# Output projection wholly in Strassen form by way of DRAM, with its operands and those of the first FFN product made in two parts; norm powers on ScalarE and the attention mask ahead of the exponential

## The chip, the cores and the metric

One core of one Trainium2 chip runs the whole layer as one program. The metric is the device time of that core in microseconds (us). Five engines work side by side, each through its own queue in order: TensorE (PE, with its weight loads as PEld), VectorE (DVE), ScalarE (ACT), GpSimd (POOL) and SyncE (SP), which here only issues DMA transfers. Operands live in SBUF, matmul results in PSUM banks, weights and spilled tensors in DRAM. All values are float32.

## The reference

512 tokens (T), a model width of 2048, one layer of a decoder with two parallel branches:

```python
h = rmsnorm(x, attn_norm_g)
proj = h @ w_in                       # u, v_sgu, q, k, v_att, g_a, g_b
u = gelu(u); v_sgu = rmsnorm(gelu(v_sgu), sgu_norm_g)
y_a = u * (tril(w_s) @ v_sgu + b_s)   # per chunk of 128 tokens
q = rmsnorm(q, q_norm_g); k = rmsnorm(k, k_norm_g)     # per head of 128
...
z = q @ k.T * Dh ** -0.5
strict = key_pos < q_pos
log_1m = where(strict, log_sigmoid(-z), 0)
tail = cumsum(log_1m, reverse=True) - log_1m
w = where(strict, exp(log_sigmoid(z) + tail), 0)
y_b = w @ v
...
merged = sigmoid(g_a) * (y_a @ w_up_a) + sigmoid(g_b) * (y_b @ w_up_b)
x = x + merged @ w_o
hid = rmsnorm(x, ffn_norm_g) @ w_ffn_in
x = x + (silu(hid[..., :HID]) * hid[..., HID:]) @ w_ffn_out
x = x + sigmoid(rmsnorm(x, ple_norm_g) @ w_ple_gate) * (p @ w_ple)
```

The changed parts are the norms of q and k, the masked weights w, `merged @ w_o` and the product with `w_ffn_in`.

## The kernel before, in words

Activations are kept transposed. A large product is cut into *forms* and *units*. A form is the moving operand of 256 rows of the contracted dimension (a `Form`, with 512 tokens); a unit, or *pair*, is 256 output columns, and walks over all forms of the product (8 for the model width). Every float32 matrix product is made of three matmuls with the operands split into a high part (ACT, a rounding copy, `whi` or `parts`) and the rest (DVE, a subtraction, `wlo` or `parts`).

For each form a unit uses one of two kinds. Kind **P** (plain): four blocks of weights, 12 matmuls of 512 columns. Kind **S** (Strassen): seven products of half blocks. Undoubled, an S form takes 21 matmuls of 256 columns (`mm3`, lines 284 to 286). *Doubled* (line 695), each product needs 7 matmuls of 512 and 7 of 256 columns, since the high part of the weight meets the high and low halves of the operand side by side; the halves are then added by `mix_doubled`. Doubling needs a PSUM bank for each product, and is used only where a unit holds no P form.

The operand of an S form needs seven blocks in place of four: the first four are those of a P form too, the other three are sums. A form can be made at once (`strassen_form`, `all_first`) or in two parts (`plain_first`): first the four blocks, with which units take it as P, and then, after a second load of the same rows, the three sums. The table `until` says for how many units a form is still taken as P. Two arenas of SBUF hold the operands: `parts` for split operands (an S form takes 3584 columns of 29,696) and `wholes` for raw ones.

What sets the order: the code walks the units, and `tick()`, called once for each form of a unit on PE, lets the other work in. At a tick at most one raw operand is fetched, one form of the list `builds` steps on, and steps that `after(n, ...)` put off come due. Weights come in through SP into four landing places, the sums of S weights by an accumulating DMA on POOL and by DVE (line 363), their high parts on ACT (line 347), their rests on DVE (line 344), into three slots; a slot is free when PE is done with the pair of forms that used it.

The stages in turn: the input projection (36 units; the attention runs beside it in four rounds), the up projections with gates (`w_up_a`, `w_up_b`, all P), the output projection (8 units `j` over the 8 forms `ms`), five small products of the per-layer embedding (`ple_pair`), FFN-in (44 units `m` over the 8 forms `fs`), FFN-out in three passes, and the last gate.

Before the change the output projection takes its forms by `OUT = "SSSSPPPP"` in each unit, from `merged[j]` in SBUF. FFN-in takes unit 0 as P and all others as doubled S, with its forms (loaded from the spilled `x1`) made at once. FFN-out already has its forms from DRAM in two parts: unit 0 all P, unit 1 half S and half P, and doubled S from unit 2 (`PLAIN_UNTIL`).

In the attention each of 32 blocks (a head and 128 keys, four rounds of eight) goes through `stage_a` (scores, logarithms), `stage_m` (DVE makes `w` and `s`, POOL masks `s`), `stage_b` and `stage_c` (split of the sums), `stage_d` (two matmuls with a triangle, `w` minus their result, exponential, POOL mask of `w`), and after four blocks `finish` (matmuls with `v`). The norms of q and k take squares on ACT, a mean on DVE, the power -0.5 on POOL, for q a factor on DVE, and scale the tokens on ACT.

## Time and profile before

| what | before |
|---|---|
| median of 3 runs | 2675.95 us (2674.31 to 2677.8) |
| the profiled execution, its own time | 2676.21 us |
| its span in the trace | 2674.5 us |
| granted TensorE clock | 0.999 |
| busy share PE, DVE, ACT, POOL | 99%, 82%, 52%, 18% |
| DMA moved | 540.25 MB, 202 GB/s over the span |
| up projections on PE | 825.8 to 1001.1 us |
| output projection on PE | 1001.1 to 1169.2 us |
| five embedding products, then FFN-in unit 0 | 1169.2 to 1182.7, to 1209.4 us |
| rest of FFN-in on PE | to 2048.7 us |

Times are read from the start of the span. Matmuls overlap on PE, so the distance between the starts of two of them is the cost of one, not its length. A unit's cost is the distance between the first matmuls of two units. A row of waits gives the engine and line that waited, for whom, the total in us, how often, and the longest.

### The profile page before, as it was taken

Reading aid. Unit: us, or ns where it says so; the run is one execution under the profiler, and the core shown is the slowest. Engines: PE = TensorE matmul, PEld = TensorE weight load, DVE = VectorE, ACT = ScalarE, POOL = GpSimd, SP = SyncE. Lnnn points to the kernel's source line nnn. Section 1 sums busy time; section 2 is a strip of 40 time slices with the busy share of each in tenths; the row PEclk is TensorE's granted clock in tenths of the full one; section 3 lists DMA queues with packets and bytes.
Section 4 is the critical chain, followed back from the end, with each engine's and each line's share of the span. In section 5 each row is a group of like instructions: output and inputs, shape, how many; then the busy total and the mean of one; then the engine's idle time right before and its main releaser. Section 6 shows DMA issues by size and latency. Waiting matters only on the chain.

```text
span 2674.5 us, 42586 instructions
## 1 busy us (share of the span) xinstructions
PE 2647.8 (99%) x15496; PEld 2322.1 (87%) x15496; DVE 2206.1 (82%) x3720; ACT 1392.0 (52%) x2171; POOL 471.2 (18%) x565
## 2 busy tenths in 40 slices
PE   8999999999999999999999999999999999999999
PEld 7889898988998889988888888888888888889898
DVE  8587878787887666678888888888889989989776
ACT  7656565665554334365444444444445445445543
POOL 0232323232220000001111111111111211211010
PEclk9999999999999999999999999999999999999999
DMA  7577777777776457668888888888788989978784
GB/s 230 151 186 175 180 173 184 173 179 201 178 187 199 141 154 210 188 213 195 220 217 206 207 202 201 204 202 206 195 208 226 263 219 272 226 238 257 242 241 132
DMA packets 285939, 540.25 MB, mean 202 GB/s; under 512 B 25632, under 2 KB 138016, under 8 KB 285728
## 3 DMA queue, kind: packets, MB, share of 16 engines
q1 hardware_dynamic: 224624, 424.25, 49.0%
q0 software_dynamic: 61104, 113.27, 27.0%
q8 instruction: 121, 1.98, 0.3%
q14 instruction: 90, 0.74, 0.1%
HBM read 490.24 MB, written 47.19 MB: 201 GB/s over the span
## 4 chain that ended last, share of the span: by engine, by line
PE 89%; DVE 5%; ACT 2%; DMA 2%; issue 1%; POOL 1%; SPq 0%; DVEq 0%; ACTq 0%; POOLq 0%
PE ps L695 48%; PE ps L286 11%; PE ps L285 11%; PE ps L284 11%; PE small L695 6%; DVE wlo L344 1%; DVE out L754 1%; PE small L1157 1%; DMA wholes<-x 1%; PE small L1032 1%; DVE wholes L363 1%; ACT whi L347 1%; DVE parts L275 0%; PE small L1107 0%; POOL wholes L1120 0%
## 5 line engine op out<-in xcount | busy, mean ns | idle before, releaser
L695 PE MATMUL ps<-parts,whi 128*128 128x512 f32 x3960 | 1324.8, 397 | 0.3 <-DVE p L754 0.3
L347 ACT ACTIVATE whi<-wholes 128x512 fp32r<-128x512 f32 (+3 forms) x933 | 866.5, 942 | 785.1 <-DVE wholes L363 270.9
L344 DVE TENSOR_TENSOR wlo<-wholes,whi 128x512 fp32r<-128x512 f32 (+3 forms) x933 | 974.4, 1078 | 82.5 <-ACT whi L347 82.1
L695 PEld LDWEIGHTS ps<-parts,wlo 128*128 128x128 f32 x3960 | 743.7, 188 | 167.8 <-issue 1.0
L695 PE MATMUL ps<-parts,wlo 128*128 128x256 f32 x3960 | 784.3, 279 | 0.1
L285 PE MATMUL ps<-parts,whi 128*128 128x256 f32 (+1 forms) x2070 | 678.3, 328 | 1.0 <-DVE parts L275 0.9
L286 PE MATMUL ps<-parts,wlo 128*128 128x256 f32 (+1 forms) x2070 | 677.9, 328 | 1.1 <-DVE wlo L344 1.1
L284 PE MATMUL ps<-parts,whi 128*128 128x256 f32 (+1 forms) x2048 | 668.0, 328 | 8.2 <-ACT parts L274 5.9
L695 PEld LDWEIGHTS ps<-parts,whi 128*128 128x128 f32 x3960 | 637.7, 189 | 6.1 <-issue 1.0
L285 PEld LDWEIGHTS ps<-parts,whi 128*128 128x128 f32 x2070 | 392.5, 190 | 41.4 <-DVE parts L275 2.5
L284 PEld LDWEIGHTS ps<-parts,whi 128*128 128x128 f32 x2048 | 388.2, 190 | 44.0 <-ACT parts L274 7.4
L286 PEld LDWEIGHTS ps<-parts,wlo 128*128 128x128 f32 x2070 | 392.8, 190 | 35.5 <-DVE wlo L344 2.3
L363 DVE TENSOR_TENSOR wholes<-wholes 128x256 f32<-128x256 f32 (+1 forms) x806 | 338.7, 420 | 21.3 <-DVE wlo L344 3.0
L754 DVE TENSOR_TENSOR out<-out,ps 128x256 f32<-128x256 f32 x460 | 190.5, 416 | 142.1 <-ACT out L751 141.8
L351 POOL DMA_DIRECT2D wholes<-w_ffn_in x172 | 150.1, 872 | 690.0 <-DVE wholes L363 268.5
L351 POOL DMA_DIRECT2D wholes<-w_in x132 | 117.8, 894 | 480.6 <-DVE wholes L363 125.9
L695 PE MATMUL small<-parts,whi 128*128 128x512 f32 x440 | 174.5, 397 | 0.0
L275 DVE TENSOR_TENSOR parts<-wholes,parts 128x1024 fp32r<-128x1024 f32 (+4 forms) x138 | 131.5, 965 | 18.9 <-ACT parts L274 18.9
L274 ACT ACTIVATE parts<-wholes 128x1024 fp32r<-128x1024 f32 (+4 forms) x138 | 113.2, 845 | 44.8 <-DVE wholes L513 25.7
L351 POOL DMA_DIRECT2D wholes<-w_ffn_out x64 | 55.9, 873 | 355.2 <-DMA wholes<-w_ffn_out 87.6
L751 ACT ACTIVATE out<-ps 128x256 f32<-128x256 f32 x243 | 91.0, 384 | 46.6 <-PE ps L695 43.3
L1403 ACT ACTIVATE out<-out 128x512 f32<-128x512 f32 x44 | 27.9, 633 | 159.6 <-DVE out L1402 159.6
(120 smaller groups left out, 1735.5 us busy)
## 6 DMA issues: line engine op xcount, KB each, us to landing
wholes<-w_ffn_in SPq DMA_DIRECT2D x172, 384.0 KB, 5.7
wholes<-w_in SPq DMA_DIRECT2D x132, 384.0 KB, 4.8
wholes<-w_ffn_in SPq DMA_DIRECT2D x172, 256.0 KB, 4.9
wholes<-w_ffn_in POOLq DMA_DIRECT2D x172, 256.0 KB, 5.4
wholes<-w_in SPq DMA_DIRECT2D x132, 256.0 KB, 4.1
wholes<-w_in POOLq DMA_DIRECT2D x132, 256.0 KB, 4.9
wholes<-w_ffn_out SPq DMA_DIRECT2D x64, 384.0 KB, 6.2
wholes<-hid SPq DMA_DIRECT2D x42, 512.0 KB, 6.1
```

The lines of the kernel that those rows point to most:

```text
L274: return (nc.scalar.activation(hi, src, AF.Copy), nc.vector.tensor_tensor(out=lo, in0=src, in1=hi.bitcast(F32), op=ALU.subtract))
L275: nc.vector.tensor_tensor(out=lo, in0=src, in1=hi.bitcast(F32), op=ALU.subtract))
L284: nc.tensor.matmul(ps, sh, mh, start=start, stop=False)
L285: nc.tensor.matmul(ps, sh, ml, start=False, stop=False)
L286: return nc.tensor.matmul(ps, sl, mh, start=False, stop=stop)
L344: in_turn(nc.vector.tensor_tensor(out=self.lo[:, blocks], in0=r, in1=h.bitcast(F32), op=ALU.subtract))
L347: in_turn(nc.scalar.activation(h, r, AF.Copy))
L351: nc.gpsimd.dma_start(out=raw[:, 3:5], in_=self.src[:, 1:3], accum_op=ALU.add)
L363: in_turn(nc.vector.tensor_tensor(out=o, in0=x, in1=y, op=ALU.add))
L695: m = nc.tensor.matmul(out, l, r, start=first and k == 0, stop=last and k == 1)
L751: in_turn(nc.scalar.activation(out, x, AF.Copy, scale=scale))
L754: in_turn(nc.vector.tensor_tensor(out=out, in0=x, in1=y, op=op))
```

## The change

- The output projection is all S: unit 0 takes its 8 forms as P, unit 1 four as S and four as P, units 2 to 7 all as S and doubled (`HALF`).
- Its operands go by way of DRAM: each `merged[j]` is stored, and a `late_form` loads it for the first four blocks and once more for the sums.
- FFN-in's forms are made in two parts in the same manner, with a second load and a second scaling by the norm's gain; its unit 1 is now half S and half P.
- `ple_operands` moves from unit 1 of the output projection to three ticks into unit 7.
- A second part is fetched only when no first part of its stage among the next three is still to be fetched, unless the form was used already.
- The norms of q and k take their power as a logarithm and an exponential on ACT; the factor of q is folded into the constants of the mean.
- The mask of `w` stands in `stage_m`, before the subtraction, with -10000 in place of 0 after the exponential.

```diff
-OUT = "SSSSPPPP"
+MASKED = -1e4
+
 PASSES = "SSSSSSSS", "SSSSSSSS", "SSSSPP"
-PLAIN_UNTIL = (1, 1, 1, 1, 2, 2, 2, 2), (1, 1, 1, 1, 2, 2, 2, 2), (2, 2, 2, 2, 1, 1)
+HALF = 1, 1, 1, 1, 2, 2, 2, 2
+PLAIN_UNTIL = HALF, HALF, (2, 2, 2, 2, 1, 1)
...
         elif seconds and fits([(wholes, 5 * 256, "old")]):
-            (urgent or seconds)[0].fetch_second()
+            f = (urgent or seconds)[0]
+            if f.used or not any(b.stage == f.stage and b.ready() and not b.there
+                                 for b in list(builds)[:AHEAD]):
+                f.fetch_second()
...
-    def token_rms(ps, r):
+    def token_rms(ps, r, scale=1.0 / P, eps=eps_cols):
 
         norm1.row()
         ms = squares(ps)
-        nc.vector.scalar_tensor_tensor(out=ms, in0=ms, scalar=1.0 / P, in1=eps_cols,
+        nc.vector.scalar_tensor_tensor(out=ms, in0=ms, scalar=scale, in1=eps,
                                        op0=ALU.mult, op1=ALU.add)
-        nc.gpsimd.tensor_tensor(out=r, in0=ms, in1=expo[:, :NT], op=ALU.pow)
+        nc.scalar.activation(ms, ms, AF.Ln)
+        nc.scalar.activation(r, ms, AF.Exp, scale=-0.5)
...
-            token_rms(ps, r)
-            nc.vector.tensor_scalar(out=r, in0=r, scalar1=float(P) ** -0.5, scalar2=None,
-                                    op0=ALU.mult)
+            token_rms(ps, r, 1.0, eps_q)
...
                 nc.gpsimd.memset(s[0:1, :P], 0.0)
+            nc.gpsimd.affine_select(out=w[:, :P], in_=w[:, :P], pattern=[[1, P]],
+                                    compare_op=ALU.is_gt, fill=MASKED, base=0,
+                                    channel_multiplier=-1)
...
             nc.scalar.activation(w, w, AF.Exp)
-            nc.gpsimd.affine_select(out=w[:, :P], in_=w[:, :P], pattern=[[1, P]],
-                                    compare_op=ALU.is_gt, fill=0.0, base=0,
-                                    channel_multiplier=-1)
...
-            plan(w_o[j], OUT)
+            plan(w_o[j], now("S" * KU, HALF, j))
...
-            plan(w_ffn_in[m], ("S" if m else "P") * KU)
+            plan(w_ffn_in[m], now("S" * KU, HALF, m))
...
+    def store(n, j, block):
+        nc.sync.dma_start(out=spill[n, j], in_=block.f())
+        there.add((n, j))
+        give(block)
+
+    ms = [spilled_form("S", "mix", j) for j in range(KU)]
+    build(ms)
...
-                merged[j] = s
-    finish_waiting()
+                after(1, lambda j=j, s=s: store("mix", j, s))
...
-    fs = [spilled_form("S", "x1", j, (g_ffn, j), twice=False) for j in range(KU)]
+    fs = [spilled_form("S", "x1", j, (g_ffn, j)) for j in range(KU)]
...
+        if j == KU - 1:
+            after(3, ple_operands)
         if j == 1:
-            ple_operands()
-            builds.extend(fs)
-        pr = pair(ms, last=j == KU - 1)
+            build(fs)
+        pr = pair(ms, last=j == KU - 1, j=j, until=HALF, doubled=7)
...
-        o = pair(fs, last=m == KH - 1, j=m, until=(1,) * KU, doubled=7).out()
+        o = pair(fs, last=m == KH - 1, j=m, until=HALF, doubled=7).out()
```

In the code after the change line numbers are other ones: 284 is the high part of an operand (274 before), 357 that of weights (347), 520 the scaling by a gain (508), 873 a copy of an embedding product out of PSUM (885), 361 the accumulating weight transfer (351), 1108 the select on `s` (1120), 1117 the select on `w` (1148), 1028 a square (1039), 1044 the scaling of tokens (1054).

POOL's queue in the attention, some blocks into the first round. Before:

```order
L351 DMA wholes<-w_in 128x512
L1148 AFFINE_SELECT wholes<-wholes 128x128
L1120 AFFINE_SELECT wholes<-wholes 128x128
L1127 COPY wholes<-wholes 1x384
L351 DMA wholes<-w_in 128x512
L1128 MEMSET wholes 1x128
```

After:

```order
L361 DMA wholes<-w_in 128x512
L1117 AFFINE_SELECT wholes<-wholes 128x128
L1108 AFFINE_SELECT wholes<-wholes 128x128
L1115 COPY wholes<-wholes 1x384
L361 DMA wholes<-w_in 128x512
L1116 MEMSET wholes 1x128
```

The rows look alike, but before, 1148 belongs to an earlier block, whose exponential it follows; after, 1117 is the mask of the very block whose select 1108 it now stands ahead of.

ACT's queue at the first norms of q and k. Before (`rr_819` is the power that POOL makes, `cols` the factors for v):

```order
L347 ACTIVATE whi_80<-wholes 128x1280
L1039 ACTIVATE sq_835,ms_834<-small_829 128x128
L347 ACTIVATE whi_80<-wholes 128x512
L1054 ACTIVATE wholes<-small_814,rr_819 128x128
L1054 ACTIVATE wholes<-small_842,cols_591 128x128 x4
L1054 ACTIVATE wholes<-small_814,rr_819 128x128 x3
```

After:

```order
L357 ACTIVATE whi_80<-wholes 128x1280
L1038 ACTIVATE ms_822<-ms_822 128x4
L1028 ACTIVATE sq_837,ms_836<-small_831 128x128
L1039 ACTIVATE rr_821<-ms_822 128x4
L357 ACTIVATE whi_80<-wholes 128x512
L1044 ACTIVATE wholes<-small_816,rr_821 128x128
L1044 ACTIVATE wholes<-small_845,cols_592 128x128 x2
```

The logarithm and the exponential (1038, 1039) stand between the high parts of weights.

ACT's queue late in unit 7 of the output projection and on into the embedding products. Before:

```order
L508 ACTIVATE wholes<-wholes,gcol 128x512
L347 ACTIVATE whi_80<-wholes 128x512
L508 ACTIVATE wholes<-wholes,gcol 128x512 x3
L274 ACTIVATE parts<-wholes 128x4x256 x2
L274 ACTIVATE parts<-wholes 128x3x256
L347 ACTIVATE whi_78<-wholes 128x512
L274 ACTIVATE parts<-wholes 128x3x256
```

After:

```order
L357 ACTIVATE whi_76<-wholes 128x512
L357 ACTIVATE whi_80<-wholes 128x512
L520 ACTIVATE wholes<-wholes,gcol 128x512 x2
L284 ACTIVATE parts<-wholes 128x512 x2
L284 ACTIVATE parts<-wholes 128x4x256
L357 ACTIVATE whi_78<-wholes 128x512
L520 ACTIVATE wholes<-wholes,gcol 128x512 x2
L739 ACTIVATE out_10710<-ps_10588 128x256
L284 ACTIVATE parts<-wholes 128x4x256
L739 ACTIVATE out_10710<-ps_10593 128x256
```

`whi_80` of 512 columns holds the weights of the first embedding product. The sums' high parts (3x256) have left this place and come later; the embedding's operands (128x512 x2) and the copies out of the doubled unit's PSUM banks (739) have come in.

76 lines of the change are left out of this document (31 added, 45 removed).

## The prediction

> **What bounds the kernel now.** First I read the page's busy times, slices and chain of waits.
>
> ```profile
> span 2674.5 us, 42586 instructions
> PE 2647.8 (99%) x15496; PEld 2322.1 (87%) x15496; DVE 2206.1 (82%) x3720; ACT 1392.0 (52%) x2171; POOL 471.2 (18%) x565
> ...
> PEclk9999999999999999999999999999999999999999
> ...
> PE 89%; DVE 5%; ACT 2%; DMA 2%; issue 1%; POOL 1%; SPq 0%; DVEq 0%; ACTq 0%; POOLq 0%
> ```
>
> PE is busy in nearly the whole span at the full granted clock, and the chain runs through it for 89%. A busy PE may still be slowed, so next I took what PE waited for, from the view of waits:
>
> ```profile
> PE ps L284 <- ACT parts L274: 5.9, 2, 4.8
> ...
> PE small L1032 <- ACT wholes L1054: 2.2, 1, 2.2
> PE small L1157 <- POOL wholes L1148: 2.2, 4, 0.6
> ...
> PE ps L284 <- ACT whi L347: 2.2, 3, 1.3
> ```
>
> These four rows make 12.5 us of 2674.5; the largest of the rest, 3.5 us at line 1142, is not touched. So two things count: how long PE needs for its matmuls, and whether PE starts to wait. Matmuls are priced by the distance between starts of units, from the timeline (PE alone) and, for doubled units, from the chain:
>
> ```profile
> 1001.10 0.28 PE L284 MATMUL ps<-parts,whi 128*128 128x256 f32 x1
> ...
> 1148.19 0.28 PE L284 MATMUL ps<-parts,whi 128*128 128x256 f32 x1
> ...
> 2048.65 0.39 PE L284 MATMUL ps<-parts,whi 128*128 128x512 f32 x1
> ...
> 2070.41 0.28 PE L284 MATMUL ps<-parts,whi 128*128 128x256 f32 x1
> ...
> 2091.76 0.39 PE L695 MATMUL ps<-parts,whi 128*128 128x512 f32 x1
> ...
> 1213.99 4.18 PE ps L695 x24
> ...
> 2034.17 4.19 PE ps L695 x24
> ```
>
> A half S, half P unit, as in all of the output projection: units 0 and 7 start at 1001.10 and 1148.19, so (1148.19 - 1001.10) / 7 = 21.01 us. A P unit of 8 forms, FFN-out's first: 2070.41 - 2048.65 = 21.76. The unit behind it is again half and half and took 21.35, so 0.34 was lost there. A doubled S unit, over 42 units of FFN-in: (2034.17 - 1213.99) / 42 = 19.53.
>
> **The change part by part.** *Matmuls of the output projection.* Before, 8 x 21.01 = 168.1. After, 21.76 + 21.01 + 6 x 19.53 = 159.95. This gives -8.1, all on the path. *FFN-in unit 1* turns from doubled S into half and half: 21.01 - 19.53 = +1.5. Together -6.65 us. The TensorE page of the Trainium skill (TensorE: Matmul & The Clock Gate, section Back-to-back issue gap) gives N/2.4 + 2.5 ns between lone matmuls; an estimate by it has units of 20.7, 19.5 and 18.2 and a sum of -5.5. The trace's units are each longer than that, and the trace decides.
>
> *DRAM round trip of the output projection's operands.* The last merged block must be stored, loaded, and split before PE comes to the eighth form of unit 0. Issues and landings from the page, and a cover row:
>
> ```profile
> wholes<-x SPq DMA_DIRECT2D x37, 512.0 KB, 5.7
> ...
> x<-wholes SPq DMA_DIRECT2D x16, 512.0 KB, 3.8
> ...
> L275 DVE TENSOR_TENSOR parts<-wholes,parts 128x1024 fp32r<-128x1024 f32 x8 | 9.6, 1221 | 0.2 <-ACT parts L274 0.2
> ```
>
> 3.8 + 5.7 for the two transfers, and four operations of about 1.2 us (gate, sum, two halves of the split), make 14.3 us. Seven P forms at 21.76 / 8 = 2.72 cover 19.0. SP stands still for the store's 3.8 us with weight loads behind it, which four landing places cover. I take +0.3, what the same pattern lost in FFN-out, with 0 and +3 as ends. The second loads of forms 3 to 7 are issued one to two units ahead of their use; the first three forms are finished during the up projections.
>
> *Load of the other engines in the doubled units.* FFN-in's steady unit, and a stretch of FFN-out, in windows (busy time and instructions of PE, PEld, DVE, ACT, POOL, then clock, DMA share, GB/s):
>
> ```profile
> 1248.50:1268.00 19.50, 19.50 (x114) 17.01 (x114) 17.27 (x32) 9.34 (x14) 4.36 (x5) 1.00 0.87 212
> ...
> 2100.00:2119.50 19.50, 19.50 (x113) 17.09 (x114) 19.14 (x36) 7.88 (x12) 4.40 (x5) 1.00 1.02 291
> ```
>
> A doubled output unit replaces FFN-in's two vector operations on the hidden half by two of the norm, and adds the sum onto x (1.22 us): DVE 18.5 of 19.53. Its transfers are FFN-in's 212 GB/s x 19.5 us = 4.1 MB, less 0.26 of hidden, plus 1.05 of x in and out: 4.9 MB or 252 GB/s. The second row shows PE without a gap at DVE 19.14 and 291 GB/s, so I take 0; the high end is the 0.34 that the unit above lost, in each of six, +2. In FFN-out and the gate the new rule lets first parts go ahead of second ones by a tick or two of 2.7 us; by the same 0.34 I give it 0, with 0.5 to each side.
>
> *Masks ahead.* At the end of a round PE waits for the mask behind the exponential; the timeline of round one:
>
> ```profile
> 189.09 0.63 ACT L1147 ACTIVATE wholes<-wholes 128x512 f32<-128x512 f32 x1 [4.97 <-DVE wholes L1146]
> ...
> 189.80 1.15 POOL L1148 TENSOR_SCALAR_AFFINE_SELECT wholes<-wholes 128x128 f32<-128x128 f32 x1 [0.21 <-ACT wholes L1147]
> ...
> 191.00 1.45 PE L1157 MATMUL small<-wholes 128*128 128x512 f32 x3 [0.54 <-POOL wholes L1148]
> ```
>
> Without the mask the exponential ends at 189.72, before PE is there; the whole 2.2 us of the four waits go. But POOL now does this mask ahead of the select on s, and what follows it (copy, memset, ACT's high part, DVE's rest, the triangle matmuls) comes later by its length. These rows bound that:
>
> ```profile
> L1148 POOL TENSOR_SCALAR_AFFINE_SELECT wholes<-wholes x32: 284/709/3865, 130.3 to 597.6; 128x128 f32<-128x128 f32 x32
> ...
> ACT parts L1131 <- POOL wholes L1128: 4.1, 4, 1.0
> ```
>
> ACT found POOL late only 4 times in 32, so 4 x 0.709 = 2.8 is the high end, 0 the low one; I take +0.7, near 0, since PE comes some us behind ACT.
>
> *Powers on ACT.* In the first round POOL was held by a weight transfer, and PE paid 2.2:
>
> ```profile
> 96.57 0.16 DVE L1047 SCALAR_TENSOR_TENSOR ms<-ms,eps_cols 128x4 f32<-128x4 f32 x1 [1.46 <-ACT sq L1039]
> ...
> 99.95 1.38 POOL L1049 TENSOR_TENSOR rr<-ms,expo 128x4 f32<-128x4 f32 x1
> 101.36 0.17 DVE L1064 TENSOR_SCALAR rr<-rr 128x4 f32<-128x4 f32 x1 [4.62 <-POOL rr L1049]
> ...
> 103.02 0.66 PE L1032 MATMUL small<-ident,wholes 128*128 128x128 f32 x4 [2.23 <-ACT wholes L1054]
> ```
>
> After, ACT makes the power in its own turn behind two weight splits; I reckon the last scaled token at about 102.1 in place of 103.7, and take -1.2 of 2.2 (ends 0 and -2.2). In other rounds PE did not wait here. The 32 small ACT instructions stand before weight splits, for which PE waited 2.2 us in all; twice that, +2, is the high end, and I take 0. The number of ACT table loads is five in both kernels.
>
> *The passage into FFN-in.* Here ACT is the engine to watch.
>
> ```profile
> 1169.20:1182.70 13.50, 13.13 (x63) 10.71 (x61) 12.28 (x20) 12.39 (x19) 0.00 (x0) 1.00 0.81 260
> 1182.70:1209.40 26.70, 25.60 (x115) 20.69 (x116) 22.02 (x39) 20.13 (x32) 6.23 (x6) 1.00 0.93 271
> ...
> 1181.75 1.05 PE L970 MATMUL small<-ones,wholes 128*128 128x1 f32 x8 [0.37 <-DVE wholes L960]
> ...
> 1203.04 0.50 PE L284 MATMUL ps<-parts,whi 128*128 128x512 f32 x1 [1.04 <-ACT parts L274]
> ...
> L274 ACT ACTIVATE parts<-wholes 128x1024 fp32r<-128x1024 f32 x8 | 8.2, 1050 | 0.0
> L508 ACT ACTIVATE wholes<-wholes,gcol 128x512 f32<-128x512 f32 x12 | 7.9, 711 | 1.3 <-DMA wholes<-x 1.3
> ...
> L885 ACT ACTIVATE out<-ps 128x512 f32<-128x512 f32 x10 | 5.5, 596 | 0.9 <-DMA ple<-out 0.9
> ...
> L347 ACT ACTIVATE whi<-wholes 128x1280 fp32r<-128x1280 f32 x4 | 5.1, 1272 | 1.5 <-PE ps L285 1.5
> L347 ACT ACTIVATE whi<-wholes 128x512 fp32r<-128x512 f32 x7 | 4.4, 628 | 3.0 <-PE ps L285 1.9 <-DVE wholes L363 1.0
> L347 ACT ACTIVATE whi<-wholes 128x1024 fp32r<-128x1024 f32 x4 | 4.2, 1058 | 0.0
> ```
>
> Before, PE waited 0.37 + 1.04 = 1.4 here. After, the weights of the first embedding product stand ahead of all form work in ACT's queue and wait for the slot of unit 7's second pair of forms, two pairs or 9.8 us into the unit. From there until unit 0 is done, ACT's queue holds (each row less the 0.1 by which neighbours overlap) 26 half gains at 0.62, 11 splits at 0.95, 10 copies of embedding products at 0.5, high parts of weights (five of 512, five of 1024, two S pairs of 1280 and 512) for 10.8, and the embedding operands, a square, the norm row and the doubled unit's copies for 3.7: 16.1 + 10.5 + 5.0 + 10.8 + 3.7 = 46.1. PE's own work is 9.7 of unit 7, 13.6 embedding products, 1.8 norm matmuls and 21.8 of unit 0, 46.9. There is no slack, and ACT also waits for slots. In detail: the copies of the third embedding product, whose banks FFN-in's first unit takes, lie behind 24.5 us of that work and some 0.7 of waiting, 15.5 us after unit 7's end, and PE is there at 13.6, which costs some 2; and I reckon the sums of form 1 about 1 us late for unit 1, since its second load follows the last embedding store on SP. The eight second loads, 4.2 MB, fall into units 0 and 1, which as P take fewer bytes of weights, so I give them nothing more. I take 3.3 of waiting in place of 1.4: +1.9. Low end: both old waits go and none comes, -1.4. High end: the five second gains that lie ahead of unit 1 show in full, 10 x 0.66 = +6.6.
>
> *The sum:* -6.65 + 0.3 + 0 - 2.2 + 0.7 - 1.2 + 1.9 = -7.15. Against the profiled execution's own 2676.21 us (1.7 beside its span) that is 2669.06; the median of the runs is 0.26 lower than that execution, so 2668.8.
>
> **The rivals.** A, the forecast: -5.35 to -9.5. B, ACT's queue at the passage eats the gain: for it, ACT is busy 20.13 of 26.7 us there before and gets 10.6 us more; against it, a part falls behind unit 1. With +6.6 there, nothing saved but the masks: -6.65 + 0.3 - 2.2 + 0.7 + 6.6 = -1.25, or 2674.7. C, the passage becomes free and both attention waits go: -6.65 - 1.4 - 4.4 = -12.5, or 2663.5; for it, x1's last first part is fetched ahead of the last embedding store now. D, slower: every mask delays its block. POOL's select took from 284 to 3865 ns for the same shape, and it now stands beside the second of the two vector operations that make w and s. If each of the 32 shows at its median, 32 x 0.709 = 22.7 us, and the sum is +14.8 with the masks' +0.7 taken off, or 2690.8; it makes the kernel slower by over 0.2% from (7.85 + 5.35) / 32 = 0.41 us a block. Against it: those 4 waits in 32. The Trainium skill (SBUF — State Buffer, section SBUF: two separate sides) says that a vector operation with two SBUF inputs and a GpSimd one lock each other out for a whole instruction; the spread of that row agrees.
>
> **How the numbers follow.** 0.2% of this kernel is 5.35 us, about what its runs can tell from no change. A 0.50, B 0.30 (-1 to -5.35), C 0.14, D 0.06. Faster by over 0.2% is A and C, 0.64; within it B, 0.30; slower D, 0.06. The range leaves out D and the outer parts of B and C: 2663.0 to 2674.8.
>
> **What would show it.** Right: output units 2 to 7 start 19.53 us apart, FFN-in's unit 1 takes 21, no PE wait for a mask. The wait before the first matmul of FFN-in and before its unit 1, with ACT as releaser, show B or C. PE waits at the triangle matmuls beyond 3 us in all would show D. A doubled unit over 20 us would mean that DVE or the weights' transfers don't keep up, which I gave no price.

## The result, and the profile after

The changed kernel takes 2668.2 us (median of 5 runs, 2664.19 to 2669.45) against 2677.8 before: a ratio of 0.9965, 95% interval 0.9954 to 0.9975, or -9.4 us. A second measurement on another occasion gave 0.9969 (0.9959 to 0.9979). The forecast was 2668.8, or -7.15 against a median of 2675.95; here the kernel before had 2677.8. So the change is within the interval of -12.3 to -6.7 us, and that the absolute times agree to 0.6 us is partly luck. Several terms under the total are not right, and the experiments are about those.

The page of the changed kernel first: span, busy times, granted clock.

```profile
span 2666.5 us, 42598 instructions
...
PE 2640.4 (99%) x15354; PEld 2312.4 (87%) x15354; DVE 2236.4 (84%) x3791; ACT 1413.9 (53%) x2245; POOL 453.4 (17%) x557
...
PEclk9999999999999999999999999999999999999999
```

It reads like the page before. The view of waits (engine, tile, line, releaser; us in total, times, longest) says more.

```profile
PE ps L294 <- ACT parts L284: 5.6, 3, 5.1
PE ps L683 <- DVE out L787: 3.1, 1, 3.1
PE small L1145 <- ACT wholes L1138: 2.5, 3, 0.8
...
PE small L1133 <- DVE parts L1126: 1.6, 4, 0.7
```

The waits for the mask and for the scaled tokens of the first round are gone. The first row was there before. The second is new: one wait of 3.1 us for line 787, the two sums that empty the banks of a mixed unit (`rest`). The third is new too: the first product of a head's finish waits for an exponential. PE's timeline shows where stages start: the up projections, output units 1 and 2, the wait, unit 3, the first embedding product, FFN-in's units 1 and 2.

```profile
820.63 0.40 PE L294 MATMUL ps<-parts,whi 128*128 128x512 f32 x1
...
1018.00 0.28 PE L294 MATMUL ps<-parts,whi 128*128 128x256 f32 x1
...
1039.01 0.39 PE L683 MATMUL ps<-parts,whi 128*128 128x512 f32 x1
...
1047.37 0.47 PE L683 MATMUL ps<-parts,whi 128*128 128x512 f32 x1 [3.09 <-DVE out L787]
...
1063.42 0.39 PE L683 MATMUL ps<-parts,whi 128*128 128x512 f32 x1
...
1161.05 0.39 PE L294 MATMUL ps<-parts,whi 128*128 128x512 f32 x1
...
1199.39 0.28 PE L294 MATMUL ps<-parts,whi 128*128 128x256 f32 x1
...
1221.46 0.39 PE L683 MATMUL ps<-parts,whi 128*128 128x512 f32 x1
```

Units 3 to 7 take (1161.05 - 1063.42) / 5 = 19.53 us, as forecast. Unit 2 takes 24.41, which is 4.88 more, though its wait is 3.1. Windows of that unit (busy time and instructions of PE, PEld, DVE, ACT, POOL, then clock, DMA share, GB/s) show the rest.

```profile
1049.00:1050.00 1.00, 1.00 (x5) 0.89 (x4) 1.00 (x4) 0.70 (x1) 0.79 (x1) 0.50 0.90 227
1050.00:1052.00 2.00, 2.00 (x9) 1.71 (x8) 1.70 (x2) 2.00 (x3) 0.10 (x1) 0.50 1.09 324
1052.00:1054.00 2.00, 2.00 (x12) 1.73 (x12) 2.00 (x5) 0.83 (x2) 0.00 (x0) 0.99 1.05 367
```

About a us after the wait PE's granted clock falls to half, for 3.4 us (1048.63 to 1052.05 in the trace's record of the clock); PE is "busy" there at half its pace, and no view of waits counts it. The same fall stands in the trace of before, behind the 2.2 us wait of the first round that the prediction quoted:

```profile
104.00:106.00 2.00, 2.00 (x10) 1.81 (x9) 0.49 (x2) 1.95 (x8) 0.47 (x1) 0.54 0.88 264
106.00:108.00 2.00, 2.00 (x13) 2.00 (x13) 0.00 (x0) 1.02 (x1) 0.94 (x1) 0.60 0.16 61
```

That is 2 x 0.46 + 2 x 0.40 = 1.7 us lost. The page can't show it: one digit of its clock row is an average over 67 us, and 9 stands for anything from 90%.

### The profile page after: what moved, and what is told of

Same layout as the page of the kernel before. It is cut to its first block, busy times and chain, and to the rows that moved or that the text cites. A ratio compares the mean times of both kernels' runs of the same rounds, so it can differ in the third digit from the quotient of the medians.

```text
span 2666.5 us, 42598 instructions
## 1 busy us (share of the span) xinstructions
PE 2640.4 (99%) x15354; PEld 2312.4 (87%) x15354; DVE 2236.4 (84%) x3791; ACT 1413.9 (53%) x2245; POOL 453.4 (17%) x557
## 4 chain that ended last, share of the span: by engine, by line
PE 88%; DVE 5%; ACT 2%; DMA 2%; issue 1%; POOL 0%; SPq 0%; POOLq 0%; DVEq 0%; ACTq 0%
PE ps L683 49%; PE ps L295 10%; PE ps L296 10%; PE ps L294 10%; PE small L683 6%; DVE wlo L354 2%; DVE out L742 1%; PE small L1145 1%; PE small L1021 1%; DMA wholes<-x 1%; DMA wholes<-w_in 1%; ACT whi L357 1%; DVE wholes L373 0%; PE small L1095 0%; DVE parts L285 0%
## 5 line engine op out<-in xcount | busy, mean ns | idle before, releaser
L683 PE MATMUL ps<-parts,whi 128*128 128x512 f32 x4200 | 1404.7, 398 | 3.7 <-DVE out L787 3.1
L683 PE MATMUL ps<-parts,wlo 128*128 128x256 f32 x4200 | 832.0, 279 | 0.0
L683 PEld LDWEIGHTS ps<-parts,whi 128*128 128x128 f32 x4200 | 676.4, 189 | 10.2 <-issue 4.5
L294 PE MATMUL ps<-parts,whi 128*128 128x256 f32 (+1 forms) x1822 | 598.9, 330 | 8.0 <-ACT parts L284 5.6
L295 PE MATMUL ps<-parts,whi 128*128 128x256 f32 (+1 forms) x1838 | 605.9, 330 | 0.8 <-DVE parts L285 0.8
L296 PE MATMUL ps<-parts,wlo 128*128 128x256 f32 (+1 forms) x1838 | 605.8, 330 | 0.0
L295 PEld LDWEIGHTS ps<-parts,whi 128*128 128x128 f32 x1838 | 348.4, 190 | 39.0 <-DVE parts L285 2.4
L294 PEld LDWEIGHTS ps<-parts,whi 128*128 128x128 f32 x1822 | 344.6, 190 | 41.5 <-ACT parts L284 6.7
L373 DVE TENSOR_TENSOR wholes<-wholes 128x256 f32<-128x256 f32 x822 | 345.1, 420 | 21.7 <-DMA wholes<-w_ffn_in 2.6
L742 DVE TENSOR_TENSOR out<-out,ps 128x256 f32<-128x256 f32 x490 | 202.9, 416 | 149.9 <-ACT out L739 149.4
L361 POOL DMA_DIRECT2D wholes<-w_ffn_in x170 | 148.0, 870 | 691.2 <-DVE wholes L373 197.4
L683 PE MATMUL small<-parts,whi 128*128 128x512 f32 x480 | 190.3, 396 | 0.0
L285 DVE TENSOR_TENSOR parts<-wholes,parts 128x1024 fp32r<-128x1024 f32 (+3 forms) x148 | 138.1, 945 | 23.0 <-ACT parts L284 23.0
L284 ACT ACTIVATE parts<-wholes 128x1024 fp32r<-128x1024 f32 (+3 forms) x148 | 119.3, 830 | 55.1 <-DVE wholes L525 33.3
```

The costliest lines, as they stand in the source:

```text
L284: return (nc.scalar.activation(hi, src, AF.Copy), nc.vector.tensor_tensor(out=lo, in0=src, in1=hi.bitcast(F32), op=ALU.subtract))
L285: nc.vector.tensor_tensor(out=lo, in0=src, in1=hi.bitcast(F32), op=ALU.subtract))
L294: nc.tensor.matmul(ps, sh, mh, start=start, stop=False)
L295: nc.tensor.matmul(ps, sh, ml, start=False, stop=False)
L296: return nc.tensor.matmul(ps, sl, mh, start=False, stop=stop)
L361: nc.gpsimd.dma_start(out=raw[:, 3:5], in_=self.src[:, 1:3], accum_op=ALU.add)
```

## Where the time went: stages of every run

Each entry is worked out from PE's first matmuls of the stages, in the one profiled execution of each run: when the up projections start; from there to the end of the output projection; its units 2 to 7 (117.2 if each takes 19.53); from there to the end of FFN-in; from there to PE's last matmul. The last column is the median of the timed runs, which need not be near the one profiled execution; the kernel before had medians of 2677.8 to 2678.9 beside them.

| kernel | up start | up + output | units 2-7 | passage + FFN-in | FFN-out to end | median |
|---|---|---|---|---|---|---|
| before | 825.8 | 343.4 | - | 879.5 | 620.3 | 2677.8 |
| powers_alone | 822.2 | 343.9 | - | 881.4 | 621.0 | 2674.3 |
| mask_alone | 824.1 | 343.8 | - | 878.5 | 621.1 | 2676.9 |
| strassen_alone | 827.1 | 344.8 | 126.0 | 880.2 | 619.9 | 2675.3 |
| changed | 820.6 | 340.4 | 122.0 | 880.6 | 619.3 | 2668.2 |
| changed_again | 818.3 | 338.9 | 120.8 | 881.1 | 618.7 | 2669.6 |
| rest_first | 821.9 | 338.0 | 119.1 | 880.8 | 620.2 | 2668.2 |
| store_apart | 820.2 | 337.4 | 119.0 | 881.2 | 625.9 | 2671.7 |
| mask_last | 818.2 | 338.9 | 120.2 | 880.9 | 620.8 | 2667.0 |
| all_three | 817.7 | 335.5 | 117.2 | 880.7 | 626.9 | 2668.8 |
| ages_alone | 821.9 | 342.2 | 124.3 | 881.0 | 627.9 | 2677.4 |
| all_three_aged | 819.2 | 335.7 | 117.2 | 882.1 | 619.0 | 2663.4 |
| ffn_in_as_before | 822.7 | 344.8 | 126.0 | 884.5 | 618.6 | 2676.0 |

How much of a difference is chance can be read from stages that are the same in two kernels. The up projections of before and strassen_alone start 1.3 us apart. In changed, changed_again, rest_first, store_apart, ages_alone and ffn_in_as_before all engines run the same instructions in the same order until then, and the start lies between 818.3 and 822.7. Of the 2.4 us between the two executions of the changed kernel, 1.7 are a fall of the clock behind an early wait of 1.8 us (0.66 and 0.50 in the windows from 24 to 28 us of the first, none in the second). So a difference of a few us in one column of two executions proves nothing by itself.

## The parts alone

**Powers on ScalarE.** The kernel before, with `Ln` and `Exp` on ScalarE in place of the power on GpSimd:

```diff
-        nc.gpsimd.tensor_tensor(out=r, in0=ms, in1=expo[:, :NT], op=ALU.pow)
+        nc.scalar.activation(ms, ms, AF.Ln)
+        nc.scalar.activation(r, ms, AF.Exp, scale=-0.5)
```

> Before, with the powers of the queries' and keys' norms on ScalarE and nothing else. Theory 1 (a wait costs twice): the 2.2 us wait for the scaled tokens in the first round goes, and with it the 3.3 us at half the granted clock that follow it in the trace of before, worth 1.65 us: -3.9 us, 2673.9, the up projections start near 821.9 in place of 825.8, and no clock below 1.00 between 100 and 110 us. Theory 2 (the prediction's term): part of the wait stays, -1.2 us, 2676.6. Theory 3: the small ACT instructions delay later exponentials, so that new waits for ACT stand at the products of the finish in each round, about 1.0 us each, and eat the gain: -0.5 to +0.5.

Measured: 2674.3, ratio 0.9984 (0.9975 to 0.9992), or -4.3 us (-6.7 to -2.1). One of its windows, and from its timeline the start of the up projections:

```profile
104.00:106.00 2.00, 2.00 (x14) 1.74 (x13) 0.16 (x1) 2.00 (x10) 0.00 (x0) 1.00 0.76 108
```

```profile
822.15 0.40 PE L284 MATMUL ps<-parts,whi 128*128 128x512 f32 x1
```

No wait, no half clock, and the up projections start 3.6 us earlier, near the 3.9 of theory 1. That start alone is within chance, but the timed runs are not: the prediction's -1.2 lies outside their interval. The waits of the finish for ScalarE did not come, so theory 3 falls.

**The mask ahead.** The kernel before, with the select on `w` ahead of the exponential:

```diff
+            nc.gpsimd.affine_select(out=w[:, :P], in_=w[:, :P], pattern=[[1, P]],
+                                    compare_op=ALU.is_gt, fill=MASKED, base=0,
+                                    channel_multiplier=-1)
...
             nc.scalar.activation(w, w, AF.Exp)
-            nc.gpsimd.affine_select(out=w[:, :P], in_=w[:, :P], pattern=[[1, P]],
-                                    compare_op=ALU.is_gt, fill=0.0, base=0,
-                                    channel_multiplier=-1)
```

> Before, with the mask moved ahead of the exponential and nothing else. Theory 1: the four waits for the mask go (0.71 us of matmul distance each, 2.8) and shorter waits at triangle products and at the first finish of a round come for 1.2: -1.6 us, 2676.2, steady rounds 135.55 us in place of 135.95. Theory 2 (the prediction's term): -2.2 + 0.7 = -1.5, the same total, but the 0.7 stands at the triangle products alone. Theory 3 (each mask delays its block): +10 or more, waits at triangle products beyond 3 us. If the 1 us wait of the finish for ACT, which the changed kernel has in each round, is there, then the mask makes it; if not, the powers do.

Measured: 2676.9, ratio 0.9988 (0.9979 to 0.9997), or -3.2 us (-5.6 to -0.8); the up projections start 1.6 us earlier. Its waits in the attention:

```profile
PE small L1158 <- ACT wholes L1151: 2.6, 3, 0.9
PE small L1033 <- ACT wholes L1055: 2.5, 1, 2.5
PE small L1146 <- DVE parts L1139: 1.1, 3, 0.4
```

No PE wait for the mask is left. The new wait of the finish for ScalarE is here and was not in powers_alone, so the mask makes it. With 0.8 us that the view puts down to issue, the finish waits 3.4 us in four rounds, where it had waited 2.2 for the mask: PE's wait there changed its cause and did not go. The triangle products wait less (1.1 in place of the 3.5 at line 1142, which the prediction held untouched), but how much less is chance: 0.9 to 3.5 in six executions that run the changed kernel's attention. The old 2.5 us wait for the scaled tokens stays, and the clock falls behind it again (0.50 in 106 to 108 us).

**Is it the place of the select?** In the changed kernel GpSimd does the select on `w` (line 1117) ahead of the one on `s` (line 1108). From its timeline, VectorE's splits of weights among them:

```profile
283.30 2.95 POOL L1117 TENSOR_SCALAR_AFFINE_SELECT wholes<-wholes 128x128 f32<-128x128 f32 x1 [0.85 <-DVE wholes L1104]
...
284.02 2.07 DVE L354 TENSOR_TENSOR wlo<-wholes,whi 128x1280 fp32r<-128x1280 f32 x2
...
286.21 0.29 POOL L1108 TENSOR_SCALAR_AFFINE_SELECT wholes<-wholes 128x128 f32<-128x128 f32 x1
```

The run mask_last puts it behind the select on `s`, the copy and the memset:

```diff
-                nc.gpsimd.memset(s[0:1, :P], 0.0)
-            nc.gpsimd.affine_select(out=w[:, :P], in_=w[:, :P], pattern=[[1, P]],
...
+                last = nc.gpsimd.memset(s[0:1, :P], 0.0)
+            in_turn(last, nc.gpsimd.affine_select(
+                out=w[:, :P], in_=w[:, :P], pattern=[[1, P]], compare_op=ALU.is_gt,
+                fill=MASKED, base=0, channel_multiplier=-1))
```

> The changed kernel, where GpSimd does the mask of w after the select on s, the copy and the memset, not ahead of them. Nothing is left out. Theory 1 (the mask delays ScalarE's high part of the sums, and the exponential of the block before stands behind that in ScalarE's queue): the wait of the finish for ScalarE, 1.0 us in each round, goes or falls below 0.4; with the shorter waits at triangle products, -2 to -4 us, steady rounds 134.6 to 135.0 us in place of 135.5. Theory 2 (ScalarE's own load makes that wait): rounds stay at 135.5, no gain. Theory 3 (the mask is now late for its own exponential): new waits for GpSimd, +1 to +3.

The same rows of mask_last, where line 1115 is the select on `w`:

```profile
282.78 2.36 POOL L1108 TENSOR_SCALAR_AFFINE_SELECT wholes<-wholes 128x128 f32<-128x128 f32 x1 [1.06 <-DVE wholes L1106]
...
282.90 2.08 DVE L354 TENSOR_TENSOR wlo<-wholes,whi 128x1280 fp32r<-128x1280 f32 x2
...
285.10 0.29 POOL L1115 TENSOR_SCALAR_AFFINE_SELECT wholes<-wholes 128x128 f32<-128x128 f32 x1
```

The wait of the finish fell from 0.8 to 0.5 us in each of the four rounds. The triangle products wait 0.6 to 0.8 in place of 0.2 to 0.7, which is within their chance; rounds take 135.4 to 135.7 us in both, and 2667.0 against 2669.6 of the changed kernel beside it is within the two intervals. Theory 2 comes nearest in time. The rows tell why little is won: a select that meets VectorE's weight splits is long wherever it stands. Here the long one ends 0.16 us after the second split (286.25 and 286.09 us; 285.14 and 284.98). Of the two selects of a block the first is the longer in 19 of 32 blocks of the changed kernel and in 16 of 32 here, so the order does not decide it.

**The Strassen part alone**: the changed kernel with powers and mask as before.

> The changed kernel with powers and mask as before, so the output projection, its way through DRAM, FFN-in's forms and the new rule of ticks alone. Theory 1 (the terms as the two traces give them): -8.15 of matmuls, +0.3, +3.1 of wait for the sums of the mixed unit and +1.65 for the half clock behind it, -1.2 at the passage, +2.5 in FFN-in's unit 1, -1.1 in FFN-out and the gate: -2.8, so 2675.0; unit 2 of the output projection takes 24.4 us, units 3 to 7 19.53. Theory 2 (the prediction's terms): -6.65 + 0.3 + 1.9 = -4.45, 2673.4, unit 2 takes 19.53 to 20. Theory 3: the wait in unit 2 is chance of one execution and half the loss: -5 to -6.

Measured: 2675.3, ratio 0.9990 (0.9981 to 0.9999), or -2.7 us (-5.1 to -0.3), near theory 1; the interval holds theory 2's -4.45 as well, so the trace must decide. In the profiled execution the wait for the sums was 5.8 us long and the half clock around its end lasted 7, so that unit 2 took 28 us, far from theory 2's 20; the up projections and the output projection together were slower than before (344.8 against 343.4). So the wait is no chance, only its length is.

The three parts add up: -4.3 - 3.2 - 2.7 = -10.2, against -9.4 and, the second time, 0.9969 or -8.3, well within the intervals, each some 2.3 us to either side.

## The wait in output unit 2

From the views of waits of SP and VectorE around unit 1 of the changed kernel, and from the timeline of the two:

```profile
SPq L516 <- DMA x<-wholes: 3.3, 1, 3.3
...
DVE wholes L525 <- DMA wholes<-mix: 3.6, 2, 1.9
```

```profile
1023.80 0.33 SPq L1376 DMA_DIRECT2D x<-wholes  x1
...
1024.71 4.63 SPq L516 DMA_DIRECT2D wholes<-mix  x2
...
1035.10 1.10 DVE L525 TENSOR_TENSOR wholes<-wholes 128x256 f32<-128x256 f32 x3 [1.94 <-DMA wholes<-mix]
...
1043.67 2.09 DVE L354 TENSOR_TENSOR wlo<-wholes,whi 128x1280 fp32r<-128x1280 f32 x2
1045.67 0.95 DVE L285 TENSOR_TENSOR parts<-wholes,parts 128x768 fp32r<-128x768 f32 x1
1046.54 1.28 DVE L787 TENSOR_TENSOR out<-ps,out 128x512 f32<-128x512 f32 x2
```

The store of unit 0's result goes out at 1023.80. A second load of a form takes the landing place that this result has just given back, so SP stands 3.3 us until the store has read it. The load lands late, VectorE stands on it, and the sums, ready to run at 1039.0, come behind form work and weight splits at 1046.54. PE needs the banks at 1047.37 - 3.09 = 1044.3. How long PE stands differs much: in five executions that run the same instructions on all engines up to there (changed, changed_again, ages_alone, gaps, ffn_in_as_before) the wait is 3.1, 3.4, 5.2, 5.0 and 5.9 us. Two kernels cut this chain at two places.

**rest_first** puts the sums ahead of the form work of the last two P forms:

```diff
-                    tick()
+                    if not (self.early and self.left["P"] < 2):
+                        tick()
+                if stop and self.early:
+                    self.rest(self.o, in_turn)
+                    for u in range(2):
+                        tick()
```

> The changed kernel with the two sums that free the mixed output unit's banks put ahead of the form work of its last two P forms in VectorE's order. Nothing is left out. Theory 1 (VectorE's queue makes the wait, and the wait makes the clock drop): both go, -3.1 - 1.65 = -4.8 us against the changed kernel, 2663.4 where that has 2668.2; unit 2 takes 19.5 to 19.8 and the clock stays at 1.00. Theory 2 (the clock drops for another reason): -3.1, unit 2 takes 21.2 with a clock of 0.93 in it. Theory 3 (transfers bound unit 2, 299 GB/s in it): the wait moves to form operands or weights and unit 2 stays at 23 to 24.4.

**store_apart** gives the place back four ticks later:

```diff
-        give(h)
+        if j == 0:
+            after(4, lambda h=h: give(h))
+        else:
+            give(h)
```

> The changed kernel, where the block of the first output unit is given back for new loads four ticks after its store was issued, not at once. Nothing is left out. Theory 1 (a chain: the second load of a form takes the block just given, SP stands 3.3 us until the store has read it, the load lands late, VectorE stands on it and the sums behind it come late): SP's wait for the store goes, VectorE's waits for the second loads go from 3.6 us to under 1, unit 2 takes 19.5 to 20.5 at full clock, -4 to -4.9 us against the changed kernel. Theory 2 (VectorE's own work is too much): the wait shrinks by less than 2 us and 1 or more stays. Theory 3 (the transfers are the bound, 299 GB/s): the loads land as late as before, unit 2 stays at 24.

The waits around unit 1, of rest_first and then of store_apart:

```profile
SPq L516 <- DMA x<-wholes: 4.1, 1, 4.1
...
DVE wholes L525 <- DMA wholes<-mix: 3.8, 2, 2.5
...
PE ps L689 <- DVE p L748: 0.7, 1, 0.7
```

```profile
SPq L516 <- DMA x<-wholes: 1.2, 1, 1.2
...
DVE wholes L525 <- DMA wholes<-mix: 2.0, 1, 2.0
...
PE ps L683 <- DVE out L787: 1.6, 1, 1.6
```

With the sums first, PE no longer waits for them, although SP and VectorE still stand as long; with the place given late, SP's wait shrinks by 2, VectorE's by 1.6, and PE's to half. Both have units 2 to 7 in 119 us and no fall of the clock there. So order and landing place both make the wait. The transfers' rate does not bound the unit: with both edits (all_three, below) the same transfers pass in units of 19.5. Yet the timed runs gain nothing: 2668.2 and 2671.7. For rest_first the -3.0 in these units is the difference to an execution with a half clock; beside changed_again, whose wait of 3.4 us had none, it is -1.7, within what one start of the program differs from another.

> The changed kernel itself once more, so that it stands beside the others on the same chip and its trace shows what is chance. Theory 1: the wait for the sums of the mixed output unit belongs to the order of the work: it comes again, 3 to 6 us long, with the clock at half behind it, and unit 2 takes 24 to 28 us; the median is 2667 to 2670. Theory 2: it was chance of one execution: unit 2 takes 19.5 to 21 and the span is 3 to 5 us shorter than 2666.5.

The wait came again, 3.4 us long, but at full clock behind it, so that unit 2 took 23.1: the wait's place is fixed, its length and the fall of the clock are not.

**Why store_apart loses.** Its table row says where: 625.9 us behind FFN-in in place of 619. It changes nothing there but the ages of the free landing places: the allocator takes the place that was given longest ago, and the order in which places were given around unit 1 still decides placings 1300 us later. The run ages_alone writes those ages into the changed kernel at the end of FFN-in, and nothing else:

```diff
+            wholes.given[:60] = [
+                t for t, n in ((128, 10), (119, 2), (121, 2), (127, 10), (133, 2), (132, 2),
+                               (123, 2), (126, 10), (129, 10), (125, 6), (130, 2), (131, 2))
+                for _ in range(n)]
             build(hs[0])
```

> The changed kernel, where only the ages of the free places in the landing arena are overwritten, once, at the end of FFN-in, by those which store_apart has there; the free places are the same in both, and nothing is left out. Theory 1 (store_apart lost 2.1 us in FFN-out and 4.7 in the gate because these ages place later loads behind one another): the same waits come here, near 2220 and 2400 us, and cost 5 to 7 us behind FFN-in: 2673 to 2675 where the changed kernel has 2668 to 2669. Theory 2 (the loss was chance of one execution): no loss, 2668 to 2669.5. Theory 3 (waits of about 1 us, and the clock's fall behind them by chance): +2 to +3.

It took 2677.4, more than expected, and behind FFN-in it lost as store_apart did, most of it in FFN-out's last pass (the expectation says the gate, whose weights come later). PE's waits there, and ScalarE's:

```profile
PE ps L294 <- ACT parts L284: 2.6, 2, 2.2
PE ps L295 <- DVE parts L285: 1.9, 2, 1.0
...
ACT wholes L520 <- DMA wholes<-x: 4.1, 1, 4.1
```

ScalarE stands 4.1 us on a load of x2 for the gate's forms, PE waits 4.5 and the clock is at half for 6.8 us; the changed kernel has no PE wait in that stretch. By the table the ages cost 8.6 to 9.2 us behind FFN-in. The three executions with store_apart's edit or its ages (store_apart, ages_alone, all_three) need 625.9 to 627.9 us there, and the other kernels with the new output projection 618.6 to 620.8, so this is no chance of one execution: the changed kernel's FFN-out is as fast as it is by the luck of a placing. By the timed runs the ages cost 5 to 6 us (0.9989 against 0.9965 and 0.9969), with no run of the changed kernel on the same occasion.

**Together.** all_three is rest_first, store_apart and mask_last; all_three_aged sets the ages back to those of the changed kernel.

> The changed kernel with the sums first (rest_first), the block apart (store_apart) and the mask last (mask_last) together. Nothing is left out. If the terms add: -4.9 for unit 2 and -2 to -4 in the attention, so 2659.5 to 2661.5 where the changed kernel has 2668.2. If the freed loads collide elsewhere, at the passage into FFN-in or in the next units: 2663 to 2667.

> all_three, with the ages of the free landing places at the end of FFN-in set to those of the changed kernel. Nothing is left out. If the loss behind FFN-in comes from the ages: unit 2 takes 19.5 us, the end lies 7 to 8 us before that of all_three, 2660 to 2662, and the profiled span is 2657 to 2660. If it does not: 2667 to 2669 as all_three.

all_three: 2668.8, units 2 to 7 in 117.2, and the same loss behind FFN-in. all_three_aged: 2663.4, ratio 0.9941 (0.9929 to 0.9954), 0.2 to 0.3% below the changed kernel's; FFN-out to the end is back at 619.0. It is still 1.4 us over the expected range; its trace has two falls of the clock, behind waits near 24 and 1169 us, which all_three has not. Its output projection:

```profile
1037.66 0.39 PE L689 MATMUL ps<-parts,whi 128*128 128x512 f32 x1
...
1154.87 0.39 PE L294 MATMUL ps<-parts,whi 128*128 128x512 f32 x1
```

(1154.87 - 1037.66) / 6 = 19.54 us for each of the six, where the prediction had 19.53 for all of them.

## The passage into FFN-in

> The changed kernel with FFN-in's forms as before (whole forms from one load, unit 1 doubled). Nothing is left out. The prediction's term: the two part forms cost 1.9 us at the passage and 1.5 in unit 1, so this is 3.4 us faster than the changed kernel, 2665. Theory 1 (from the traces: 38.3 us from the end of the output projection to unit 1 with two part forms in three executions, 39.5, 41.5 and 38.7 with whole forms; unit 1 22.0 in place of 19.5): the passage takes 39 to 41, unit 1 19.5, together -1 us or nothing, 2667 to 2669. Theory 2 (the shorter passage comes from the new output projection, not from the forms): the passage stays at 38.3, -2.5 us, 2666.

```diff
-            plan(w_ffn_in[m], now("S" * KU, HALF, m))
+            plan(w_ffn_in[m], ("S" if m else "P") * KU)
...
-    fs = [spilled_form("S", "x1", j, (g_ffn, j)) for j in range(KU)]
+    fs = [spilled_form("S", "x1", j, (g_ffn, j), twice=False) for j in range(KU)]
```

All three missed: 2676.0, ratio 0.9993 (0.9985 to 1.0002), some 7 us slower than the changed kernel by the ratios. Only a part of that comes from the edit. PE runs the same instructions as in the changed kernel up to the end of the output projection, and 126.0 us for units 2 to 7 in place of 120.8 to 124.3 is the chance length of the wait for the sums. The passage with FFN-in took 884.5 us in place of 880.6 and 881.1. PE's waits from output unit 2 to FFN-in's unit 1:

```profile
PE ps L683 <- DVE out L787: 5.9, 1, 5.9
PE ps L294 <- ACT out L873: 2.4, 1, 2.4
PE small L932 <- DVE diag L930: 1.3, 1, 1.3
```

The clock fell to half at the end of the first and behind the second. The wait for the copies of the third embedding product (line 873) is the one that the prediction feared for the changed kernel; that has 0.6 there. So the two part forms relieve the passage, by one execution of this kernel: behind the new output projection whole forms made passage and FFN-in 3.4 to 3.9 us slower, not 3.4 faster as the prediction's term has it, and slower than in the kernel before (879.5). What the whole forms hold up first, ScalarE's queue or a landing place, these rows don't tell.

## A wait and the clock

> The changed kernel with 36 waits of TensorE built into FFN-in's units 4 to 39, of 1 to 6 ACT operations each; nothing is left out. It asks from which length on a wait makes the granted clock fall. Theory 1 (a threshold near 2 us): every wait over 2 us is followed by 3 us at 0.5, none under 2 is. Theory 2 (a window that runs free): between 1.5 and 3.5 us some waits are followed by it and some are not, over 3.5 all of them. Each such fall costs some 1.65 us more.

The built-in waits, 36 in one execution, sorted by the distance between the starts of the two built-in matmuls:

| distance, us | 0.64 | 1.30 | 1.96 | 2.62 | 3.29 | 3.95 |
|---|---|---|---|---|---|---|
| waits | 6 | 6 | 6 | 6 | 6 | 6 |
| followed by half clock | 0 | 0 | 0 | 3 | 5 | 6 |

The 22 units behind a wait without a fall took 19.83 to 19.85 us up to the next built-in matmul. Behind a wait with one they took 1.5 to 1.6 us more where the half clock lasted 3.4 us, and 2.4 to 2.8 more where it lasted 6.8. One long wait, and a window behind it:

```profile
1309.66 0.80 PE L1420 MATMUL small<-wholes,ident 128*128 128x128 f32 x2 [3.67 <-ACT wholes L1419]
```

```profile
1311.00:1313.00 2.00, 2.00 (x8) 1.71 (x8) 2.00 (x3) 0.81 (x2) 0.00 (x0) 0.50 0.65 108
```

Theory 2 holds: up to 2 us none, from 2.6 some, near 4 all. In the other traces falls came behind waits of 1.8 us (in the first 25 us of the changed kernel) to 5.9, and none behind the 3.4 of changed_again.

The record of the clock shows what decides. In each execution every fall begins on a grid of steps of 3.41 us, and lasts one or two of them; the two falls of the changed kernel, at 24.64 and 1048.63 us, lie 300 steps apart. Here are the step before that second fall and the one after it, and two steps of changed_again that share its wait (1041.70 to 1045.08) between them:

```profile
1045.22:1048.63 3.41, 1.26 (x8) 1.18 (x9) 3.41 (x6) 0.00 (x0) 0.89 (x1) 1.00 0.86 233
1048.63:1052.05 3.42, 3.42 (x14) 2.94 (x13) 3.12 (x6) 2.74 (x3) 0.88 (x1) 0.50 1.00 279
```

```profile
1039.91:1043.32 3.41, 1.79 (x10) 1.21 (x8) 3.41 (x7) 2.09 (x4) 0.26 (x1) 1.00 1.06 348
1043.32:1046.73 3.41, 1.65 (x10) 1.52 (x11) 3.41 (x6) 0.00 (x0) 0.69 (x2) 1.00 0.77 198
```

The first number behind the length is PE's busy time: in the changed kernel 3.41 - 1.26 = 2.15 us of idle time fell into one step; in changed_again 1.62 and 1.76 into two, and the clock stayed. Over the steps at full clock of all 14 traces, each of the 30 with over 1.77 us idle was followed by half clock, of the 17 with 1.6 to 1.77 only two were, and of the other 10,800 none. So what counts is how much of a wait falls into one step, and where the steps lie against a wait changes from execution to execution. Matmuls of one column counted as idle here: in all_three_aged a wait of 1.0 us and the eight 128x1 matmuls behind it, from 1168.6 to 1170.8 us, were followed by a fall.

## The prediction, point by point

- **Matmuls of the output projection, -8.1, and the round trip through DRAM, +0.3: right.** From the start of the up projections to unit 1, 1018.00 - 820.63 = 197.4 us, as the terms give (175.3 + 21.76 + 0.3), and units 3 to 7 of 19.53. all_three_aged shows them whole: 335.7 against 343.4 is -7.7, where the two terms make -7.8.
- **Load of the other engines in the doubled units, 0 with +2 at the high end: the step that failed most.** It cost 3.1 us of wait and 1.8 behind it at half clock in the profiled execution, and 3.6 to 9 in all in others. The load as such was no bound, as the prediction had it from windows; an average over a unit can't show that one short operation, the sums of the mixed unit, stands behind a burst of form work and a late load. "A doubled unit over 20 us" was named as the sign, without a price; its reading there, that VectorE or the transfers don't keep up, is not what the runs show, since order and landing place alone bring the units back to 19.54.
- **Masks, -2.2 + 0.7: right in total, not in mechanism** (-1.6 by the up projections' start, -3.2 (-5.6 to -0.8) by the timed runs). The waits of 2.2 us at the finish did not go: the exponential now comes later, and PE waits 3.4 for it. The view of waits shows the gain at the triangle products, where the prediction had a loss. Over 3 us of waits there, its sign for D, was no test, since the kernel before has 3.5.
- **Powers, -1.2 of 2.2: sized too small.** The whole wait went, and with it 1.7 us of half clock that was in the trace of before and that the prediction read over ("at the full granted clock"): -3.6 in the trace, -4.3 by the timed runs.
- **Passage, +1.9, and FFN-in's unit 1, +1.5: too dear together.** From the end of the output projection to that of FFN-in, changed, changed_again and strassen_alone need 880.6, 881.1 and 880.2 us; before, powers_alone and mask_alone 879.5, 881.4 and 878.5: +0.8 in the mean, not +3.4. Up to the end of unit 1 PE waits 0.6 us for the third embedding product's copies and 0.5 besides, in place of 1.4. ScalarE had no slack by the sum of its rows, but unit 1 paid (1221.46 - 1199.39 = 22.07, not 21.01), not the passage; waits make half of that 1.06, and the rest stays open.
- **FFN-out and the gate, 0: -1.0** in the profiled execution; ages_alone shows that this stage moves by up to 9 us with the placing.
- **The rivals.** B (ScalarE at the passage) and D (every mask delays its block) did not happen. The time landed on A because -2.4 to -3 that was missed at the powers and -2.6 at the passage stood against +3 to +5 that was missed in unit 2. In the two profiled executions the stages of the table differ by -5.1, -3.0, +1.1 and -1.0 us, where the terms give -2.7, -7.8, +3.4 and 0. That the sum came out is luck; in the attention and at the passage the kernel came nearer to C, and unit 2 brought it back.

## What to carry to other kernels

Where a wait of about 2 us or more goes or comes, look at the clock in 2 us windows behind it; a fall cost 1.5 to 2.8 us on top of the wait here, and whether it came differed between executions. A clock row averaged over tens of us hides it. Where forms are made in two parts, look at what stands behind the burst of late work in each queue, and which buffer a load must wait for: here a store's buffer, a load, VectorE's order and PE stood in one chain. And where an allocator picks places by age, an edit in one stage shifts transfers in all later ones: compare the later stages before a small gain or loss is put down to the edit, and know from a second execution of the same kernel how far each stage moves by chance.

## What was not expected of the hardware

The clock: no fall behind 18 built-in waits of up to 1.96 us, 3 of 6 at 2.62, 5 of 6 at 3.29, 6 of 6 at 3.95; falls begin on a grid of 3.41 us, and over 1.77 us of idle time in one step was followed by one each time. The Trainium skill (TensorE: Matmul & The Clock Gate, section What's actually happening) states that the clock is halved behind an idle window of about 3.4 us that runs free. The grid agrees with a window of that length which runs free; that the whole window must be idle does not, since 1.78 of 3.41 us were enough; here the measurement decides.

A 128x128 select on GpSimd took 2.95 and 2.36 us beside two-input operations of VectorE, and 0.29 right behind them. Each of the 14 attention selects of the changed kernel over 0.9 us, and of the 15 of mask_last, ended 0.13 to 0.16 us after the end of a VectorE operation with two inputs in SBUF. The Trainium skill (SBUF — State Buffer, section SBUF: two separate sides) has the two locking each other out, and these rows agree for the select, which waits; that VectorE waits for a select they don't show.
